# A linear-attention layer: second-half gate rows from stored product forms of x, and keys turned by VectorE and HBM

## The chip, the cores and the metric

The kernel runs on one core of a Trainium2 chip, in one launch. A core has TensorE (PE, matrix products into PSUM), VectorE (DVE), ScalarE (ACT), GpSimd (POOL) and SyncE (SP), which work side by side and wait for each other by semaphores, and DMA queues that move data between HBM and the on-chip SBUF. Times are device microseconds.

## The reference, cut to what matters

One layer of gated linear attention and one squared-ReLU MLP over 1024 tokens of width 1024, all in float32 (`DEPTH` is 1, so the second kind of mixer is not computed).

```
h = rms_norm(x, norm_mix)
q, k, v, r, gk_low = split(h @ w_in)          # 512, 512, 1024, 1024, 16 columns
log_a = log_sigmoid(gk_low @ w_gk_up + b_gk) / 16
# per head (4 heads, 128 key and 256 value columns), in chunks, with a state:
#   b = cumsum(log_a) in the chunk
#   o = (q*exp(b)) @ state + causal(q k^T with decay exp(b_i - b_j)) @ v
#   state = state * exp(b_last) + (k*exp(b_last - b))^T @ v
o = rms_norm(o, g_onorm) * silu(r)
x = x + o @ w_out
x = x + square(relu(rms_norm(x, norm_ffn) @ w_ff1)) @ w_ff2
out = rms_norm(x, final_norm)
```

## The kernel before

**Products by seven forms.** Every large product of float32 is written as three matmuls on a high and a low part: ACT rounds an operand to the high part and DVE subtracts it to give the low part (`split`, lines 79 to 82; in the profile L81 and L82). A 1024 x 1024 by 1024 x 512 product is not formed from eight block products but from seven, of sums and differences of blocks (`form`, lines 149 to 170; the sums are L186). So a plan's entry, for instance "wqk by x", is seven *steps* of 48 matmuls of 128x512 each (`step`, line 234). `PLAIN` is the order in which the seven forms are taken: 0, 5, 1, 2, 3, 4, 6; a position in that order is called *at*, the form's number *n*. Position 5 holds form 4, position 4 holds form 3, and so on. Form 3 of x is its block 22 (second half of the rows of x transposed, second half of the tokens); with the late order that is used here, form 4 of x is block 22 minus block 12. Forms 0 and 5 of x are blocks 11 and 21, the first half of the tokens.

**Plans.** `chunks_of` (line 278) runs three entries: i = 0 is q and k, i = 1 is v, i = 2 is r. While PE works on a step, ACT and DVE make the operands of the next one. `turns` gives the order in which that is done for a position: "x" and "w" are sums, "X" and "W" splits, "n" the sums for the weight side of the position after. `hooks` call other work at a position: `(i, at)` before the next operands are made, `(i, at, "then")` after that and ahead of the step's matmuls, and `(i, at, lane, kp)` between the matmuls of a step.

PE's instructions run in the order in which the program states them. The other engines' order is made by a scheduler at compile time, from priorities (program order, with raised priority for evictions) and estimated times; `order_after(..., wait=False)` fixes an order on one engine. Each engine then works through its own list in order.

**x in other plans.** Plan 0 makes the forms of x; all but 0 and 5 are stored to HBM as high and low parts (`keep`) and loaded again for v and r (`KeptX`, L520).

**PSUM and SBUF.** There are three PSUM banks tagged `mm` and five tagged `gl`. Products of form 5 and of forms 1, 2, 3 use three `mm` banks and one `gl` bank. SBUF tiles come from tagged pools: `big` (8) holds operands, `g4` (6) mixed tiles, `wup` (1) the split of `w_up`.

**The gates.** The gate weights are 16 columns; `split_gate` writes their high and low parts into one 128-column operand, `wgs`, four groups of (high, low), so that one matmul gives all needed partial rows (`gk_rows`, line 449). For the first half of the tokens this is done at (0, 1), from forms 0 and 5 of x: 16 matmuls (`gk_first`), and ACT copies the rows out of their bank (`gk_first_out`, L831). For the second half block 12 of x is loaded again (`x12_load`), scaled and split (`x12_split`, L371 and L374), and 16 matmuls run in plan 1 in two parts at position 5 (`gk_second`). `spread_rms` multiplies the rows by the tokens' norms, `gate_in` multiplies by `w_up`, `gate` and `prep_fast` (L562 to L583) form the cumulative decays and scale q and k by them. POOL copies two small pieces (`top`, L577, and `est`, L581) in each `prep_fast`, and ACT's exponential at L579 overwrites what `top` was copied from.

**The chunks.** After the plans comes a loop over eight chunks of 128 tokens. Chunk c states, in this order: `operands(c + 1)` (q k^T of the next chunk, and the four heads' keys turned by four PE transposes into an `mm` bank, line 657, and split into `kd`), a part of r's last products (`r_part`, L804 and `silu`), `outputs(c)` (L717 to L726), `new_state(c)` (uses `kd`; L696, and POOL's L699) and `outputs_T(c - 1)` (PE transposes of the normed outputs, L736, and ACT's L738). Then come the output projection and the MLP, which the change does not touch. The MLP turns x by DVE blocks of 32x32 and stores to HBM in runs of 128 bytes (`turn_blocks`, L1001, and `turn_store`, L1008).

`general` names a second version of the whole that runs only if the decays are too strong (`flag`); here it does not.

Of the kernel before, what the change touches and what calls it, by code (L numbers as in the profile page):

```python
# [48 lines left out]
def hybrid_trunk(ctx: ExitStack, tc: tile.TileContext, x, xT, w_head, w_r, w_gk, w_up,  # L49
# [15 lines left out]
    def f32(ap):  # L65
        return ap.bitcast(F32)
# [54 lines left out]
    def run(general):  # L121
# [310 lines left out]

        wgr3 = wgr.rearrange("p (k r) -> p k r", r=16)
        wgs5 = wgs.rearrange("p (k g b r) -> p k g b r", k=8, g=4, b=2)
# [14 lines left out]
        def gk_rows(pg, kts, part, start, stop):  # L449

            for kt in kts:
                for hl in range(2):
                    mm(pg, wgs[:, kt * P:(kt + 1) * P], part(kt, hl), start and kt == kts[0] and hl == 0,
                       stop and kt == kts[-1] and hl == 1)
            return pg
# [21 lines left out]
        def qk_into(n, lane, p_):  # L477
            d = qk_view(int(PART[n][0]) - 1, lane)[:, half(int(PART[n][1]) - 1)]
            with tc.high_priority():
                if n in (3, 4, 5):  # L480
                    op = dve.tensor_tensor(d, p_, d, op=ALU.add)
                    if n == 5 and lane:
                        order_after(tc, op, last["s1" if lane == 1 else "s1_low"], wait=False)
                else:
                    op = act.activation(d, p_, AF.Copy)
                    if n == 0:
                        order_after(tc, op, last["split"], wait=False)
# [16 lines left out]
        class KeptX:  # L504
# [9 lines left out]
            def split(self, n):  # L514
                out = self.tiles[n] = [kl(new("big", F32R)) for _ in range(2)]
                for kh in range(2):
                    if n in self.again:
                        split(out[kh][:, :, 0, :], out[kh][:, :, 1, :], xq.blocks["21" if n else "11"](2 * kh, 2))
                    else:
                        nc.sync.dma_start(out[kh].rearrange("p k l t -> p (k l t)").bitcast(F32), xv[n][kh])  # L520
                if n in self.again:
                    keep(n, out)
                return out

        def spread_rms(hf):
# [10 lines left out]
            w_ = new("g4")  # L536
            dg, rbc = w_[:, 512:1024], w_[:, 0:512]
# [3 lines left out]
            raw, gk = box["raw"][hf], box["gk"][:, half(hf)]  # L541
            dst = raw if hf == 0 else dg
            dve.tensor_tensor(dst, raw, rbc, op=ALU.mult)
            act.activation(gk, dst, AF.Copy)
            dve.tensor_tensor(gk[64:128, :], dst[64:128, :], f32(gk[64:128, :]), op=ALU.subtract)
# [26 lines left out]
        def prep_fast(h, hf):  # L572
# [10 lines left out]
            dve.tensor_tensor(kh, a_, kh, op=ALU.mult)  # L583

# [54 lines left out]
        def operands(c, bank_tag="gl"):  # L639
# [15 lines left out]
            kp = new(bank_tag)  # L655
            for h in range(H):
                pe.transpose(kp[:, h * P:(h + 1) * P], qk_view(1, h)[:, c * P:c * P + P], ident)  # L657
# [156 lines left out]
        xq.first = lambda n, kh: scale_x(kh, *{5: ("21",), 1: ("11", "12"), 2: ("22",)}.get(n, ()))  # L814
# [8 lines left out]

        def gk_first():
            pg = gk_rows(new("mm"), range(KT), lambda kt, hl: xlive[0 if kt < 4 else 5][kt % 4 // 2][:, kt % 2, hl, :], True, True)
            box["raw"] = [pg]

        def gk_first_out():
            u, pg = new("g4"), box["raw"][0]
            box["raw"] = [u[:, 0:512]]  # L830
            act.activation(u[:, 0:512], pg, AF.Copy)  # L831

        def x12_load():
            box["x12"] = [new("raw"), new("g4")]
            for kh in range(2):
                nc.sync.dma_start(box["x12"][kh].rearrange("p (k t) -> p k t", k=2), x_piece(2 * kh, 2, 1))

        def x12_split():
            for kh in range(2):
                raw, hi, lo = box["x12"][kh], new("g4", F32R), new("g4" if kh else "raw", F32R)  # L840
                for k in range(2):
                    scaled_split(hi[:, half(k)], lo[:, half(k)], raw[:, half(k)], 2 * kh + k)
                box["x12"][kh] = hi, lo

        def gk_second(part):
            if part == 0:
                box["raw"].append(gk_rows(new("mm"), range(4, KT), lambda kt, hl: xk.tiles[3][kt % 4 // 2][:, kt % 2, hl, :], True, False))
            else:
                gk_rows(box["raw"][1], range(4), lambda kt, hl: box["x12"][kt // 2][hl][:, half(kt % 2)], False, True)
# [13 lines left out]
        hooks = {(0, 1): (gk_first,), (0, 1, "then"): (gk_first_out,), (0, 3): (split_up,),  # L863
                 (0, 4): (g(token_rms, range(0, 4)),), (0, 5): (g(token_rms, range(4, 8)),),
                 (1, 0, 0, 3): (g(spread_rms, 0),),
                 (2, 4): (r_last,),
                 (1, 2): (x12_load,), (1, 4): (x12_split,), (1, 5): (g(gk_second, 0),),
                 (1, 5, 3, 3): (g(gk_second, 1),), (1, 6, 0, 1): (g(spread_rms, 1),)}
        if not general:
            hooks.update({(1, 0, 2, 3): (g(gate_in, 0, 0, "mm"), g(gate_in, 1, 0, "mm")),  # L870
                          (1, 0, 3, 3): (g(gate_in, 2, 0, "mm"),),
                          (1, 1, 0, 1): (g(gate_in, 3, 0, "mm"), g(prep_fast, 0, 0)),
                          (1, 2): (x12_load,),
                          (1, 2, "then"): (g(prep_fast, 1, 0),), (1, 3, "then"): (g(prep_fast, 2, 0),),
                          (1, 4): (), (1, 4, "then"): (g(prep_fast, 3, 0), x12_split),
                          (1, 5): (g(gk_second, 0),),
                          (1, 6, 3, 1): (g(gate_in, 0, 1, "mm"), g(prep_fast, 0, 1)),
                          (2, 0, 0, 0): (g(gate_in, 1, 1, "mm"), g(prep_fast, 1, 1)),
                          (2, 0, 0, 2): (g(gate_in, 2, 1, "mm"),), (2, 0, 1, 0): (g(gate_in, 3, 1, "mm"),),
                          (2, 0, 3, 3): (g(prep_fast, 2, 1),), (2, 3, "then"): (g(prep_fast, 3, 1),),  # L880
                          (2, 4, 2, 1): (g(operands, 0, "mm"),)})
        chunks_of([(wqk, xq, 0, qk_into, PLAIN), (xk, wv, 1, v_into, PLAIN), (xr_, wR, 1, r_into, R_FIRST)], ops_a, hooks, {},
                  turns={(0, 1): ("X", split_gate, "W"), (0, 2): ("x", "X", "w", "W", lambda: last.update(sums=last["split"], s1=last["sum"], s1_low=last["low"]), "n"),
                         (0, 3): ("W", "x", "X", "n"), (2, 3): ("x", "X", "W", g(wR.sums, 3))})

        last_v = box["v"]

# [8 lines left out]
        for c in range(TT):  # L896
            if c == 4 and not general:
# [3 lines left out]
                dve.tensor_scalar(over[:, 1:2], over[:, 0:1], RANGE, None, op0=ALU.is_gt)  # L901
                pf = new("gl")
# [23 lines left out]
            if c:  # L926
                outputs_T(c - 1)

# [311 lines left out]
```

## Time and profile before

| | us |
|---|---|
| median of three runs | 996.23 |
| lowest and highest | 995.94, 997.4 |
| the profiled execution | 996.73 |
| its span in the profile | 995.0 |

The profile shows one execution. A row of a timeline gives start, duration, engine, line, operation, output and input tiles with their shapes and, in square brackets, the idle time of the engine before it and what ended that. Ends of matmuls are modelled, so a row of PE lasts a little longer than the time to the next row's start. L70 is the line of the helper that records every matmul, so that matmuls are told apart by their tiles: `gl<-big,big` and `mm<-big,big` are steps, `mm<-big,g` and `mm<-g,g` or `mm<-raw,g` the gate rows, `mm<-hq,hq` the chunk's q k^T, `gl<-wb,wa` and `gl<-g,hq` its outputs and states. In the chain of waits, a row is a start, a duration and an instruction; "issue" is time in which an engine waited for nothing that the profile shows.

### The profile page before, as it was taken

The numbers are of one execution on the slowest core, as the hardware profiler recorded it, in microseconds if no ns is written. First come the engines' busy times: TensorE is split into PE (matmuls) and PEld (weight loads), VectorE is DVE, ScalarE is ACT, GpSimd is POOL, SyncE is SP. The second block draws the span as 40 slices with busy tenths as digits, with TensorE's granted clock in tenths as the row PEclk, the third lists the DMA queues.
The fourth block names the chain that finished last, engine by engine and source line by source line (L and its number), as shares of the span: only waits on it lengthen the run. The fifth ranks groups of instructions, "written<-read, shape, count | busy, mean of one in ns | idle before, by whom it ended". The sixth has DMA issues, their size and how long they took to land.

```text
span 995.0 us, 12256 instructions
## 1 busy us (share of the span) xinstructions
PE 983.5 (99%) x4508; PEld 820.4 (82%) x4508; DVE 748.7 (75%) x912; ACT 564.1 (57%) x860; POOL 237.0 (24%) x146
## 2 busy tenths in 40 slices
PE   9999999999999999999999999999999999999996
PEld 7788888889988888888888888888888888888885
DVE  5996796768899999699662359974339966569976
ACT  7785564887894376666524446332447433566455
POOL 3000010213440000224042142233133224242270
PEclk9999999999999999999999999999999999999998
DMA  9899786575373257651225993367683225971004
GB/s 271 313 319 380 282 295 215 212 242 196 118 280 108 85 196 312 254 221 33 84 99 206 298 303 89 83 175 260 223 324 100 65 63 212 365 283 49 1 1 173
DMA packets 135693, 193.65 MB, mean 195 GB/s; under 512 B 39240, under 2 KB 100808, under 8 KB 124104
## 3 DMA queue, kind: packets, MB, share of 16 engines
q1 hardware_dynamic: 135064, 192.37, 56.0%
q8 instruction: 37, 0.61, 0.3%
q10 hardware_dynamic: 560, 0.40, 0.1%
q14 instruction: 32, 0.26, 0.1%
HBM read 146.62 MB, written 46.14 MB: 194 GB/s over the span
## 4 chain that ended last, share of the span: by engine, by line
PE 92%; DMA 2%; DVE 2%; ACT 2%; SPq 1%; issue 1%; DVEq 0%; ACTq 0%
PE gl L70 61%; PE mm L70 30%; DMA wb<-in_w_head 1%; DMA wa<-in_w_head 1%; DVE vx L1096 0%; PE mm L657 0%; DVE big L82 0%; ACT g L717 0%; PE mm L736 0%; ACT wb L81 0%; SPq L337 0%; DVE big L804 0%; PE gl L736 0%; DVE g L1137 0%; DVE g L726 0%
## 5 line engine op out<-in xcount | busy, mean ns | idle before, releaser
L70 PE MATMUL gl<-big,big 128*128 128x512 f32 x2700 | 626.4, 389 | 0.7 <-DVE big L82 0.4
L70 PEld LDWEIGHTS gl<-big,big 128*128 128x128 f32 x2700 | 506.5, 188 | 106.5 <-DVE big L82 1.1
L70 PE MATMUL mm<-big,big 128*128 128x512 f32 (+1 forms) x1248 | 291.7, 387 | 0.0
L70 PEld LDWEIGHTS mm<-big,big 128*128 128x128 f32 x1248 | 232.7, 188 | 48.2 <-ACT g L831 0.5
L82 DVE TENSOR_TENSOR big<-wa,big 128x1024 fp32r<-128x1024 f32 (+1 forms) x118 | 155.2, 1335 | 85.6 <-ACT big L81 84.6
L81 ACT ACTIVATE big<-wa 128x1024 fp32r<-128x1024 f32 (+1 forms) x118 | 119.2, 1039 | 127.5 <-PE gl L70 67.0
L186 POOL TENSOR_TENSOR wa<-wa,wb 128x1024 f32<-128x1024 f32 x14 | 42.0, 3011 | 299.9 <-DVE big L82 205.9
L186 POOL TENSOR_TENSOR wa<-wa,wa 128x1024 f32<-128x1024 f32 x28 | 80.0, 2866 | 132.8 <-DVE big L82 132.1
L82 DVE TENSOR_TENSOR big<-wb,big 128x1024 fp32r<-128x1024 f32 x50 | 64.4, 1305 | 27.8 <-ACT big L81 27.8
L81 ACT ACTIVATE big<-wb 128x1024 fp32r<-128x1024 f32 x50 | 51.1, 1054 | 56.8 <-PE gl L70 26.6
L82 DVE TENSOR_TENSOR big<-hq,big 128x1024 fp32r<-128x1024 f32 x48 | 61.5, 1290 | 26.7 <-ACT big L81 26.6
L82 DVE TENSOR_TENSOR big<-raw,big 128x1024 fp32r<-128x1024 f32 x42 | 67.6, 1630 | 4.9 <-ACT big L81 4.9
L81 ACT ACTIVATE big<-hq 128x1024 fp32r<-128x1024 f32 x48 | 48.7, 1052 | 39.4 <-PE gl L70 19.5
L81 ACT ACTIVATE big<-raw 128x1024 fp32r<-128x1024 f32 x42 | 43.4, 1055 | 37.9 <-DVE raw L186 17.8
L186 POOL TENSOR_TENSOR wa<-wb,wa 128x1024 f32<-128x1024 f32 x14 | 41.1, 2947 | 39.7 <-DVE big L82 39.7
L577 POOL COPY top<-g 128x4 f32<-128x4 f32 x8 | 10.1, 1267 | 167.8 <-DVE g L569 167.8
L1030 ACT ACTIVATE hq<-hq 128x1024 f32<-128x1024 f32 x24 | 25.3, 1056 | 40.9 <-DVE hq L1023 40.9
L699 POOL TENSOR_SCALAR g<-g,est 128x256 f32<-128x256 f32 x28 | 29.2, 1059 | 52.2 <-DVE g L696 33.3
L1021 ACT ACTIVATE hq<-gl 128x512 f32<-128x512 f32 x36 | 21.4, 593 | 30.6 <-PE gl L70 30.6
L70 PE MATMUL gl<-wb,wa 128*128 128x256 f32 x180 | 32.1, 310 | 0.0
L1023 DVE TENSOR_TENSOR hq<-gl,hq 128x512 f32<-128x512 f32 x24 | 16.0, 685 | 19.8 <-PE gl L70 19.8
L1068 DVE TENSOR_TENSOR vx<-gl,vx 128x512 f32<-128x512 f32 x44 | 29.1, 679 | 0.9 <-PE gl L70 0.8
(206 smaller groups left out, 898.7 us busy)
## 6 DMA issues: line engine op xcount, KB each, us to landing
big<-xw SPq DMA_DIRECT2D x42, 1024.0 KB, 6.9
big<-xv SPq DMA_DIRECT2D x20, 1024.0 KB, 6.4
xv<-big SPq DMA_DIRECT2D x14, 1024.0 KB, 8.5
xw<-big SPq DMA_DIRECT2D x14, 1024.0 KB, 4.3
wa<-in_w_ff SPq DMA_DIRECT2D x32, 256.0 KB, 4.0
wb<-in_w_ff SPq DMA_DIRECT2D x32, 256.0 KB, 3.9
wa<-in_w_ff SPq DMA_DIRECT2D x16, 512.0 KB, 6.6
wb<-in_w_ff SPq DMA_DIRECT2D x16, 512.0 KB, 5.5
```

The costliest lines, as they stand in the source:

```text
L70: pe.matmul(o, w, m, start=start, stop=stop, skip_group_check=partial)
L81: last["split"] = act.activation(hi, src, AF.Copy)
L82: last["low"] = dve.tensor_tensor(lo, src, f32(hi), op=ALU.subtract)
L186: op = self.eng.tensor_tensor(*(self.ap(b, kp, 2) for b in (o, x_, y_)), op=op)
L577: pool.tensor_copy(top[:, 8 * h + 4 * hf:8 * h + 4 * hf + 4].unsqueeze(2), a[:, :, P - 1:P])
L699: pool.tensor_scalar(S[:, vs], Z[:, vs], g, None, op0=ALU.mult)
L1021: act.activation(d, p_, AF.Copy)
L1023: dve.tensor_tensor(d, p_, d, op=ALU.add)
L1030: act.activation(d2, d2, AF.Relu)
L1068: dve.tensor_tensor(yd, p_, yd, op=ALU.add)
```

## The change

1. *Second-half gate rows.* `x12_load`, `x12_split` and `gk_second` are gone. Since W1 x12 + W2 x22 = (W1 + W2) x22 - W1 (x22 - x12), the rows are formed from the forms 3 and 4 of x that plan 0 holds anyway. `split_gate_again`, called at (0, 4, "then"), makes W1 + W2 and -W1 by two DVE operations on 128x64 values, ordered behind the last low half made by then, and splits them into a second operand. The 16 matmuls stand at (0, 5), ahead of that step's 48.
2. *The copies.* The first gate rows are copied out (`gk_out`) between the scalings of x for position 2, and the four copies of plan 0's first product wait until the x operand of position 2 is split (`qk_first_out`).
3. *Earlier gates.* `spread_rms` for the second half moves from position 6 of plan 1 to its position 0, and `gate_in` and `prep_fast` of both halves move to earlier positions.
4. *The keys.* At the end of each `prep_fast` DVE transposes the scaled keys in 32x32 blocks (128x512) into the tile of the decays. Four DMAs, begun by GpSimd one or more positions later, store it to HBM in runs of 128 bytes, so that a row there is a token with 512 values. A chunk's 128 rows are loaded by SyncE into the one `wup` tile; `operands` splits that, and its four PE transposes and their `mm` bank are gone.
5. The reduction of `top` moves from chunk 4 to chunk 2.

```diff
-        def split_gate():
+        def split_gate(wgs, wgr3):
+            wgs5 = wgs.rearrange("p (k g b r) -> p k g b r", k=8, g=4, b=2)
             for g in range(4):
                 split(wgs5[:, :, g, 0, :], wgs5[:, :, g, 1, :], wgr3)
+
+        def split_gate_again():
+            t = wgu[:, 128:256]
+            for op in (dve.tensor_tensor(t[:, 0:64], wgr[:, 0:64], wgr[:, 64:128], op=ALU.add),
+                       dve.tensor_scalar(t[:, 64:128], wgr[:, 0:64], -1.0, None, op0=ALU.mult)):
+                order_after(tc, op, last["low"], wait=False)
+            box["wgs"] = new("g4", F32R)
+            split_gate(box["wgs"], t.rearrange("p (k r) -> p k r", r=16))
...
+        def gk_out(hf):
+            if hf == 0:
+                box["raw"] = new("g4")
+            act.activation(box["raw"][:, half(hf)], box["pg"], AF.Copy)
...
-                    op = act.activation(d, p_, AF.Copy)
-                    if n == 0:
-                        order_after(tc, op, last["split"], wait=False)
+                    act.activation(d, p_, AF.Copy)
+
+        def qk_first_out():
+            for d, p_ in box["q0"]:
+                order_after(tc, act.activation(d, p_, AF.Copy), last["split"], wait=False)
...
             dve.tensor_tensor(kh, a_, kh, op=ALU.mult)
+            turn_keys(h, hf, a_)
...
+        def turn_keys(h, hf, u):
+            dve.transpose(u, qk_view(1, h)[:, half(hf)])
+            kmoved[h, hf] = u
+
+        def store_keys(h, hf):
+            u = kmoved.pop((h, hf))
+            for q_ in range(4):
+                dst = km[hf * 512:hf * 512 + 512, h * P + 32 * q_:h * P + 32 * q_ + 32].rearrange("(b i) j -> i b j", i=32)
+                pool.dma_start(dst, u[32 * q_:32 * q_ + 32, :].rearrange("p (b j) -> p b j", j=32))
+
+        def load_keys(c):
+            krows[c] = new("wup")
+            box["keys"] = nc.sync.dma_start(krows[c], km[c * P:(c + 1) * P, :])
...
-            kp = new(bank_tag)
-            for h in range(H):
-                pe.transpose(kp[:, h * P:(h + 1) * P], qk_view(1, h)[:, c * P:c * P + P], ident)
+            if general:
+                kp = new(bank_tag)
+                for h in range(H):
+                    pe.transpose(kp[:, h * P:(h + 1) * P], qk_view(1, h)[:, c * P:c * P + P], ident)
+            else:
+                kp = krows.pop(c)
...
-        hooks = {(0, 1): (gk_first,), (0, 1, "then"): (gk_first_out,), (0, 3): (split_up,),
-                 (0, 4): (g(token_rms, range(0, 4)),), (0, 5): (g(token_rms, range(4, 8)),),
-                 (1, 0, 0, 3): (g(spread_rms, 0),),
-                 (2, 4): (r_last,),
-                 (1, 2): (x12_load,), (1, 4): (x12_split,), (1, 5): (g(gk_second, 0),),
-                 (1, 5, 3, 3): (g(gk_second, 1),), (1, 6, 0, 1): (g(spread_rms, 1),)}
+        hooks = {(0, 1): (lambda: gk_rows(wgs, (xlive[0], xlive[5])),),(0, 3): (split_up,), (0, 4, "then"): (split_gate_again,),
+                 (0, 4): (g(token_rms, range(0, 4)),), (0, 5): (g(token_rms, range(4, 8)), lambda: gk_rows(box["wgs"], (xlive[3], xlive[4]))),
+                 (0, 5, "then"): (g(gk_out, 1),),
+                 (1, 0, 0, 3): (g(spread_rms, 0),), (1, 0, 1, 3): (g(spread_rms, 1),),
+                 (2, 4): (r_last,)}
...
+            for i, at, f in ((1, 1, (store_keys, 0, 0)), (1, 2, (store_keys, 1, 0)), (1, 3, (store_keys, 2, 0)), (1, 4, (store_keys, 3, 0)),
+                             (1, 6, (store_keys, 0, 1)), (2, 0, (store_keys, 1, 1)), (2, 1, (store_keys, 2, 1)), (2, 2, (store_keys, 3, 1)),
+                             (2, 2, (load_keys, 0))):
+                hooks[i, at, "then"] = (g(*f), *hooks.get((i, at, "then"), ()))
...
+            if c + 2 < TT and not general:
+                load_keys(c + 2)
```

More of the change, by code (lines that the diff above doesn't have):

```diff
@@ L447, in run, with gk_rows @@
         box = {}
-        def gk_rows(pg, kts, part, start, stop):
-            for kt in kts:
+        def gk_rows(wgs, forms):
+            box["pg"] = new("mm")
+            for kt in range(KT):
                 for hl in range(2):
-                    mm(pg, wgs[:, kt * P:(kt + 1) * P], part(kt, hl), start and kt == kts[0] and hl == 0,
-                       stop and kt == kts[-1] and hl == 1)
-            return pg
+                    mm(box["pg"], wgs[:, kt * P:(kt + 1) * P], forms[kt // 4][kt % 4 // 2][:, kt % 2, hl, :],
+                       kt + hl == 0, kt + hl == KT)
+        def gk_out(hf):
+            if hf == 0:
+                box["raw"] = new("g4")
+            act.activation(box["raw"][:, half(hf)], box["pg"], AF.Copy)
         def token_rms(ts):
@@ L519, in split @@
                     else:
-                        nc.sync.dma_start(out[kh].rearrange("p k l t -> p (k l t)").bitcast(F32), xv[n][kh])
+                        last["xv"] = nc.sync.dma_start(out[kh].rearrange("p k l t -> p (k l t)").bitcast(F32), xv[n][kh])
                 if n in self.again:
@@ L535, in spread_rms @@
                 mm(pb, ones_r, u[:, half(l)], l == 0, l == 1)
-            w_ = new("g4")
-            dg, rbc = w_[:, 512:1024], w_[:, 0:512]
+            rbc = new("g4")[:, 0:512]
             act.activation(rbc, pb, AF.Copy)
@@ L540, in spread_rms @@
                 box["gk"] = new("g4", F32R)
[L541 to L545, printed above, removed]
+            raw, gk = box["raw"][:, half(hf)], box["gk"][:, half(hf)]
+            dve.tensor_tensor(raw, raw, rbc, op=ALU.mult)
+            act.activation(gk, raw, AF.Copy)
+            dve.tensor_tensor(gk[64:128, :], raw[64:128, :], f32(gk[64:128, :]), op=ALU.subtract)
         def chunks(ap):
@@ L812, in run, with x_first @@
         xq_split = xq.split
-        xq.first = lambda n, kh: scale_x(kh, *{5: ("21",), 1: ("11", "12"), 2: ("22",)}.get(n, ()))
+        def x_first(n, kh):
+            if (n, kh) == (1, 1):
+                gk_out(0)
+            scale_x(kh, *{5: ("21",), 1: ("11", "12"), 2: ("22",)}.get(n, ()))
+        xq.first = x_first
         def remember(n):
@@ L822, in run @@
         xk, xr_ = KeptX((0, 5)), KeptX()
[L824 to L849, printed above, removed]
         wv = weight_side(True, from_v, dve, late=True)
@@ L869, in run @@
         if not general:
             hooks.update({(1, 0, 2, 3): (g(gate_in, 0, 0, "mm"), g(gate_in, 1, 0, "mm")),
[L871 to L880, printed above, removed]
+                          (1, 0, 3, 3): (g(gate_in, 2, 0, "mm"), g(prep_fast, 0, 0)),
@@ L884, in run @@
                          (0, 3): ("W", "x", "X", "n"), (2, 3): ("x", "X", "W", g(wR.sums, 3))})
         last_v = box["v"]
+        if not general:
+            load_keys(1)
         for t in range(4):
@@ L896, in run @@
         for c in range(TT):
-            if c == 4 and not general:
+            if c == 2 and not general:
                 over = new("st")
@@ L901, in run @@
                 dve.tensor_scalar(over[:, 1:2], over[:, 0:1], RANGE, None, op0=ALU.is_gt)
+            if c == 4 and not general:
                 pf = new("gl")
```

12 lines of the change are left out of this document (10 added, 2 removed).

## The prediction

> **What bounds the kernel now.** I read the page first, then the busy time by stretches, the timelines of the engines around each place that the change touches, and the chain of waits. All times are microseconds.
>
> ```profile
> span 995.0 us, 12256 instructions
> PE 983.5 (99%) x4508; PEld 820.4 (82%) x4508; DVE 748.7 (75%) x912; ACT 564.1 (57%) x860; POOL 237.0 (24%) x146
> ...
> PE 92%; DMA 2%; DVE 2%; ACT 2%; SPq 1%; issue 1%; DVEq 0%; ACTq 0%
> ```
>
> TensorE (PE) carries 92% of the chain that ends last. A change can gain only by taking instructions off PE, or by ending one of its few waits; it loses wherever PE waits for something new. So I look at the stretches in which another engine is nearly as full.
>
> ```profile
> 33.00:66.00 33.00, 32.65 (x145) 26.83 (x144) 32.89 (x33) 25.75 (x38) 0.00 (x0) 1.00 0.82 314
> ...
> 128.00:160.00 32.00, 32.00 (x143) 26.51 (x142) 27.23 (x44) 14.78 (x22) 3.76 (x7) 1.00 0.90 297
> ...
> 260.00:300.00 40.00, 39.80 (x258) 35.62 (x257) 36.28 (x81) 35.28 (x96) 16.79 (x16) 1.00 0.66 225
> ```
>
> The columns are the stretch, its length, then busy time and count of PE, weight load, VectorE (DVE), ScalarE (ACT) and GpSimd (POOL), the granted clock, the DMA share and GB/s. The clock is 1.00 in all three, so it plays no part. From 33 to 66, in the q and k projection, DVE is busy for 32.89 of 33.00. From 128 to 160, in the v projection, only DMA is near its limit (0.90). From 260 to 300, in the attention's chunks, DVE and ACT are at nine tenths. These three places decide the matter.
>
> **The start (6 to 34).** The change puts the copy of the first gate rows ahead of the scaling of two x blocks, and the four copies of q's and k's first product behind them, on ACT.
>
> ```profile
> 17.77 3.79 PE L70 MATMUL mm<-big,g 128*128 128x512 f32 x16
> ...
> 22.75 4.58 PE L70 MATMUL mm<-big,big 128*128 128x512 f32 x18
> ...
> 28.56 4.24 PE L70 MATMUL mm<-big,big 128*128 128x512 f32 x18
> 32.64 0.61 PE L70 MATMUL gl<-big,big 128*128 128x512 f32 x2
> 33.61 1.19 PE L70 MATMUL gl<-big,big 128*128 128x512 f32 x4 [0.35 <-DVE big L82]
> ...
> 65.93 24.64 PE L70 MATMUL gl<-big,big 128*128 128x512 f32 x108
> ```
>
> The last row gives the pace: 24.64 / 108 = 0.228 a matmul, so 48 of them, one step, take 10.95, and 16 gate rows 3.65. Against that pace two waits stand here. The 18 at 22.75 take 4.58 where the 18 at 28.56 take 4.24: 0.34, spent on the third `mm` bank, which holds the gate rows until ACT copies them. Between 32.64 and 33.61 two matmuls need 0.46 of 0.97: 0.51 of waiting for the low half of a weight operand on DVE.
>
> ```profile
> 20.65 2.04 ACT L485 ACTIVATE hq<-gl 128x512 f32<-128x512 f32 x4
> 22.56 2.57 ACT L366 ACTIVATE vx<-vx,vec 128x512 f32<-128x512 f32 x4
> ```
>
> ```profile
> 24.00 2.44 DVE L186 TENSOR_TENSOR raw<-vx,vx 128x1024 f32<-128x1024 f32 x2 [1.62 <-issue]
> ...
> 32.34 2.35 DVE L82 TENSOR_TENSOR big<-wa,big 128x1024 fp32r<-128x1024 f32 x2
> ```
>
> DVE idles 1.62 until the first two scalings (L366) are through; these stood behind the four copies (L485, 2.04). With the copies behind, DVE starts up to 1.62 earlier, its low halves at 32.34 come earlier too, and the bank is copied some 2 earlier. Both waits go: up to 0.85 gained, at least 0 if the weight blocks' landing holds DVE anyway. I take 0.8. The copies go into a gap of ACT; what comes next late is at 65.93.
>
> **The second gate rows (at 65.93).** Sixteen matmuls leave the v projection, and sixteen stand ahead of the step that starts at 65.93: PE's count is unchanged. Removed as well are a reload of 1 MB of x and its four scalings and four low halves, none of which PE waited for. New is a wait. The second set of gate weights is formed by two small DVE operations, which are ordered behind the last low half of this step's x operand, then four ACT copies and four DVE subtractions; PE cannot pass the gate rows to begin the step.
>
> ```profile
> 65.38 1.22 DVE L82 TENSOR_TENSOR big<-vx,big 128x1024 fp32r<-128x1024 f32 x1
> ```
>
> ```profile
> L81 ACT ACTIVATE g<-g 128x128 fp32r<-128x128 f32 x4 | 0.9, 294 | 0.0
> ...
> L82 DVE TENSOR_TENSOR g<-g,g 128x128 fp32r<-128x128 f32 x4 | 0.9, 277 | 0.0
> ```
>
> Before, the step could begin at 65.93 on the first half of the operand, with the second half (65.38 to 66.60) still in the making. Now PE waits for 66.60, plus about 0.5 for the two operations of half that width (bounded by 277 ns each), plus 0.9 for the copies, plus 0.28 for the last subtraction: 68.3, a wait of 2.3. If DVE is 1.62 ahead from the start and PE 0.85, it is 2.3 - 1.62 + 0.85 = 1.5. I take the middle, 1.9. The bounds: 0, if DVE gets so far ahead that its evictions and this operand are done before PE; 3.5, if one more low half (1.22) is put ahead of the small ones. Behind the waiting PE nothing else is late: each following step has 3.65 more time for its operands. On ACT the four copies hold up the squares of x's rows, which are needed only by the v projection.
>
> **The keys (96 to 220).** Eight DVE block transposes, 32 stores begun by GpSimd and eight loads on SyncE's queue are added; 32 PE transposes go.
>
> ```profile
> L1001 DVE STREAM_TRANSPOSE g<-g 128x1024 f32<-128x1024 f32 x8 | 9.9, 1236 | 3.1 <-DMA g<-xh 3.1
> ```
>
> ```profile
> L1008 SPq DMA_DIRECT2D xm<-g x32: 302/563/4391, 543.5 to 704.0; - x32
> ```
>
> ```profile
> xm<-g SPq DMA_DIRECT2D x32, 128.0 KB, 7.5
> ...
> raw<-xv SPq DMA_DIRECT2D x16, 256.0 KB, 3.4
> ```
>
> A transpose of half that width costs about 0.62, eight of them 5.0 of DVE, in a stretch where DVE has 4.8 free of every 32 (128 to 160) and where the low halves just removed gave time back: hidden. The stores have the form of the later `xm` stores, runs of 128 bytes, half as many each. No GpSimd store is in this trace. From SyncE's issue it would be 0.56 (0.30 to 4.39); from GpSimd's own copies in this stretch up to 3.98 (row below). I take 1.3 each, nearer to SyncE's row, so about 5 for the four of a head, inside a step of 10.95. Queued behind them on POOL are the copies of `top` and `est`, and ACT's next exponential waits for the former.
>
> The stores' bytes meet the kept x operands on the DMA engines:
>
> ```profile
> L520 SPq DMA_DIRECT2D big<-xv x2: 339/522/705, 139.9 to 143.7; - x2
> ...
> DMA to landing us min/median/max: 7.0/7.2/7.5
> ```
>
> ```profile
> 158.00 1.52 PE L70 MATMUL gl<-big,big 128*128 128x512 f32 x6
> ```
>
> These loads, begun by 143.7, have landed by 151.2, and the step that needs them starts at 158.00. That is 6.8 of cover, about as much as a load takes; while it holds, the stores cost nothing, and without it a load twice as slow would cost 0.7 a step. The key loads (256 KB like `raw<-xv`, 3.4) have one buffer: the next starts when the last is split, in a chunk of some 9.7. Hidden, if they land within 6.
>
> **The chunks (220 to 299).** Here PE loses its work.
>
> ```profile
> L657 PE MATMUL mm<-ident,hq 128*128 128x128 f32 x32 | 4.9, 276 | 0.1
> ```
>
> ```profile
> 272.26 0.74 ACT hq L738 x2
> 273.00 0.04 issue
> 273.04 0.66 PE mm L657 x4
> ...
> 282.77 0.44 PE mm L657 x4
> ...
> 296.73 1.58 DVE g L726 x4
> 298.31 0.04 issue
> 298.36 0.33 PE mm L736
> ```
>
> On the chain, four transposes take 0.44 where they run freely; eight groups make 3.5. At 273.04 they take 0.66, because their `mm` bank came late from ACT (L738); such waits, 0.2 at two places, go with the bank: 3.9 in all. Not all of it need arrive. The stretch ends with PE waiting for DVE's normed outputs (L726, to 298.31), and DVE's round is as long as PE's:
>
> ```profile
> 266.67 0.69 DVE L804 TENSOR_TENSOR big<-mm,big 128x512 f32<-128x512 f32 x1 [0.39 <-PE mm L70]
> ...
> 270.15 0.75 DVE L749 SCALAR_TENSOR_TENSOR big<-big,tok 128x512 f32<-128x512 f32 x1 [1.20 <-ACT big L748]
> ...
> 276.82 0.68 DVE L804 TENSOR_TENSOR big<-mm,big 128x512 f32<-128x512 f32 x1
> ```
>
> One round of DVE, 266.67 to 276.82, is 10.15 with 1.20 of idle for ACT in it; PE's, 273.04 to 282.77, is 9.73. PE's becomes 9.3. DVE can follow as far as its idle time, 0.39 and 1.20 a round, was PE's doing. I take 3.2, nearer to the full 3.9 since each round holds more idle than the 0.44 asked for; the least is 1.3, three early chunks at 0.44, if the later ones keep DVE's pace. The key's split reads SBUF instead of PSUM:
>
> ```profile
> L81 ACT ACTIVATE wb<-vx 128x512 fp32r<-128x512 f32 x16 | 10.2, 635 | 0.0
> ...
> L81 ACT ACTIVATE wa<-mm 128x512 fp32r<-128x512 f32 x8 | 4.7, 588 | 0.0
> ```
>
> That is 0.05 more a chunk on ACT, off PE's path.
>
> **The sum.** -0.8 + 1.9 - 3.2 = -2.1. The profiled execution took 996.73 (span 995.0 and 1.7 around it), so 994.6; it lies 0.5 above the median of 996.23, from which the change gives 994.1. About 0.2%, 2.0, is what a measurement of this kernel can tell from no change: under 994.2 counts as faster, over 998.2 as slower.
>
> **The rivals.** First, DVE holds the chunks: the loop gives only 1.3, and the sum is -0.8 + 1.9 - 1.3 = -0.2, 996.0, no change. For it speaks the chain's end on L726 at 298.31; against it DVE's idle time in each round. Second, the gate weights come as late as they can (3.5) while the loop gives all: -0.8 + 3.5 - 3.9 = -1.2, 995.0, no change either; with the weak loop and no gain at the start it is 0 + 3.5 - 1.3 = +2.2, 998.4, slower. Third, and slower by much: the stores hold up POOL.
>
> ```profile
> 184.42 3.98 POOL L577 COPY top<-g 128x4 f32<-128x4 f32 x1 [1.67 <-DVE g L569]
> ```
>
> This copy of 128x4 values lasts 3.98, while DVE runs operations without a pause. If each store takes as long, four take 15.9 of a step of 10.95; the next head's `top` copy is 5.0 later at each of six heads, ACT stops at its exponential with the next weights' splits behind it, and PE is late by 6 x 5.0 less the 6.8 of cover: 996.2 - 2.1 + 23.2 = 1017. It decides from 10.95 / 4 = 2.7 a store on. Against it: it was one copy in sixteen, and a store reads no SBUF values with GpSimd. [...]
>
> **How the numbers follow.** The forecast, with the loop's gain near 3.2 and the wait near 1.9 or less, has 0.47 and is faster; its own range is 991.5 to 994.2. No change by either way has 0.33. Slower has 0.20: 0.12 for POOL's stores, 0.08 for the late weights with a weak loop. The range of 991.5 to 998.5 goes from the best of all bounds (-0.85 + 0 - 3.9 = -4.75) to the 998.4 of the second rival, and leaves out POOL's case and a few mishaps.
>
> **What would show it.** Right: 18 matmuls in 4.24 at 22.75 and no wait at 33; a gap of PE between 65 and 68, ended by DVE's 128x128 subtractions; no L657 rows outside the fallback, a chunk of 9.3 to 9.5, and the end of the chunks some 3 earlier than the shifts at the start and at 65.93 alone would put it; POOL's stores well under 2.7 each. Wrong: PE idle between 96 and 220, ACT waiting for POOL at L579 by several microseconds, or DVE and ACT waiting in the chunks for the landing of keys.

## The result and the profile after

| us | before | after |
|---|---|---|
| median (5 runs each) | 996.23 | 1001.57 |
| lowest and highest | 995.7, 997.4 | 1000.17, 1003.05 |
| the profiled execution | 996.73 | 1002.46 |
| its span | 995.0 | 1000.7 |

The ratio is 1.0053, with a 95% interval of 1.0039 to 1.0068. The change made the kernel slower by 5.3, where 2.1 faster was forecast; 1001.57 is outside the forecast's range of 991.5 to 998.5. First the page of the kernel after:

```profile
span 1000.7 us, 12293 instructions
PE 980.9 (98%) x4476; PEld 817.4 (82%) x4476; DVE 750.4 (75%) x922; ACT 562.9 (56%) x861; POOL 259.0 (26%) x178
...
PE 87%; DVE 5%; ACT 2%; DMA 2%; issue 1%; SPq 1%; DVEq 0%; ACTq 0%
```

TensorE has its 32 instructions less and is busy 2.6 less than before (983.5), yet it carries only 87% of the chain that ends last, and DVE has 5% in place of 2%. So TensorE waits for something new. Its timeline names the places (start, duration, shapes, count, idle time before and what ended it):

```profile
17.75 4.16 PE L70 MATMUL mm<-big,g 128*128 128x512 f32 x16
...
23.12 4.24 PE L70 MATMUL mm<-big,big 128*128 128x512 f32 x18
...
33.73 1.20 PE L70 MATMUL gl<-big,big 128*128 128x512 f32 x4 [0.47 <-DVE big L82]
...
61.97 4.24 PE L70 MATMUL mm<-big,big 128*128 128x512 f32 x18
69.55 5.53 PE L70 MATMUL mm<-big,g 128*128 128x512 f32 x16 [3.34 <-DVE g L82]
74.91 5.38 PE L70 MATMUL gl<-big,big 128*128 128x512 f32 x23
...
103.94 0.51 PE L70 MATMUL mm<-g,ones_r 128*128 128x512 f32 x1 [0.96 <-DVE g L553]
...
267.54 0.38 PE L70 MATMUL gl<-st,ones 128*128 128x1 f32 x2 [1.42 <-DVE g L735]
```

The 18 matmuls at 61.97 are through, at 0.228 each, at 66.07; before, the step began at 65.93. The second gate rows begin only at 69.55: a gap of 3.5. And the 16 rows reach to 74.91, 5.36 where 16 x 0.228 = 3.65 was due. The busy time by stretches says why (length, PE, weight load, DVE, ACT, POOL, then the granted clock):

```profile
66.00:69.50 3.50, 0.21 (x1) 0.00 (x0) 3.50 (x11) 1.86 (x5) 0.00 (x0) 1.00 1.04 382
69.50:75.00 5.50, 5.45 (x17) 4.35 (x18) 3.17 (x3) 2.12 (x2) 0.00 (x0) 0.69 0.97 362
75.00:96.00 21.00, 21.00 (x95) 17.38 (x94) 14.36 (x33) 12.63 (x20) 0.00 (x0) 1.00 0.88 334
```

In the gap PE is busy for 0.21 of 3.50 and DVE for all of it; in the 5.5 behind it the granted clock is 0.69, then 1.00 again. The rows are slow because the clock is.

The chunk loop did gain. Its length is the time from the first q k^T of chunk 0 to the first matmul of the output projection, before and after:

```profile
220.59 1.05 PE L70 MATMUL mm<-hq,hq 128*128 128x128 f32 x8
...
298.88 11.14 PE L70 MATMUL gl<-big,big 128*128 128x512 f32 x48
```

```profile
227.15 1.05 PE L70 MATMUL mm<-hq,hq 128*128 128x128 f32 x8
...
302.45 11.14 PE L70 MATMUL gl<-big,big 128*128 128x512 f32 x48
```

78.29 became 75.30. So the two executions differ thus: 0.1 at the start, 3.5 of gap, 1.7 of slow rows, 1.0 at 104 and 0.3 not assigned make the 6.56 by which the loop starts later. The loop gives back 2.99, net of the new wait of 1.42 at 267 that stands in it; 3.57 remain and stay. The last outputs are issued 3.58 apart, by ScalarE's queue, before and after:

```profile
988.92 0.38 ACTq L1129 DMA_DIRECT2D out_y<-hq  x1
```

```profile
992.50 0.38 ACTq L1150 DMA_DIRECT2D out_y<-hq  x1
```

But the spans end at 995.0 and 1000.7: 6.1 and 8.2 behind those issues. Another 2.1 arise where no engine computes. 6.56 - 2.99 + 2.1 = 5.7, the difference of the spans.

### The profile page after: what moved, and what is told of

It is laid out like the page before. It is cut to its first block, busy times and chain, and to the rows that moved or that the text cites. A ratio compares the mean times of both kernels' runs of the same rounds, so it can differ in the third digit from the quotient of the medians.

```text
span 1000.7 us, 12293 instructions
## 1 busy us (share of the span) xinstructions
PE 980.9 (98%) x4476; PEld 817.4 (82%) x4476; DVE 750.4 (75%) x922; ACT 562.9 (56%) x861; POOL 259.0 (26%) x178
## 4 chain that ended last, share of the span: by engine, by line
PE 87%; DVE 5%; ACT 2%; DMA 2%; issue 1%; SPq 1%; DVEq 0%; ACTq 0%
PE gl L70 59%; PE mm L70 28%; DVE big L82 2%; DMA wb<-in_w_head 1%; ACT big L81 1%; DVE wa L186 0%; DVE vx L1117 0%; DMA vec<-in_vecs 0%; DMA vx<-in_xT 0%; DVE hq L496 0%; ACT g L756 0%; DVE raw L186 0%; PE mm L775 0%; SPq L337 0%; DVE g L765 0%
## 5 line engine op out<-in xcount | busy, mean ns | idle before, releaser
L594 POOL COPY top<-g 128x4 f32<-128x4 f32 x8 | 11.2, 1399 | 123.0 <-DVE g L586 123.0
```

The lines of the kernel that those rows point to most:

```text
L594: pool.tensor_copy(top[:, 8 * h + 4 * hf:8 * h + 4 * hf + 4].unsqueeze(2), a[:, :, P - 1:P])
```

## The experiments

My theory: TensorE's gap for the second gate weights and the low clock behind it cost 5.2, the late spreading of the norms (L553, at 104) costs 1, the keys gain 3 in the loop, and the end costs 2.1. The rival: the keys' stores and loads cost the time, and the gap would only move.

**e1: the second gate weights one step earlier.**

```diff
-        hooks = {... (0, 4, "then"): (split_gate_again,),
+        hooks = {... (0, 3, "then"): (split_gate_again,),
...
```

> One change to the kernel after: the second gate weights are formed one step earlier, behind step (0,3)'s operands. Theory: TensorE stood idle from 66.05 to 69.55 for these weights and ran the 16 gate rows behind it at a granted clock of 0.67 (5.36 us in place of 3.65); with the weights there early no wait is left at 66 and the rows take 3.65, so about 5 us less than the kernel after: 996 to 997. Rival (the loss lies in GpSimd's stores and the keys' traffic): the wait goes, but DVE's late halves only move it, and the time stays near 1001.5.

Measured: 998.96, ratio 1.0027 (1.0017 to 1.0036). TensorE's timeline of e1:

```profile
65.02 3.87 PE L70 MATMUL mm<-big,g 128*128 128x512 f32 x16
...
98.34 0.51 PE L70 MATMUL mm<-g,ones_r 128*128 128x512 f32 x1 [1.77 <-DVE g L553]
99.95 0.50 PE L70 MATMUL mm<-g,ones_r 128*128 128x512 f32 x1 [1.10 <-DVE g L553]
100.29 4.49 PE L70 MATMUL gl<-big,big 128*128 128x512 f32 x12
```

The gap at 66 is gone and the rows run at full pace: that part of the theory holds. But most of the gain is lost again at 98, since TensorE now arrives earlier and DVE does not: the diagonal blocks for the second spreading are 1.77 and 1.10 late, and the 12 matmuls behind them take 4.49 in place of 12 x 0.228 = 2.7. That is 4.6 where the kernel after lost 0.96, so only 1.5 of the 5.2 is left; another 2.0 goes at the end, where the span closes 6.2 behind the last issue in place of 8.2. The stretches of e1 show the clock at work a second time:

```profile
96.60:100.30 3.70, 0.86 (x3) 0.50 (x4) 3.25 (x11) 1.32 (x2) 0.00 (x0) 1.00 0.74 312
100.30:104.80 4.50, 4.50 (x14) 3.56 (x13) 1.38 (x2) 1.23 (x2) 0.00 (x0) 0.62 0.01 5
```

**e2: the gap filled with work.**

```diff
+            wgu_s = first_wgs
...
             box["pg"] = new("mm")
+            for _ in range(fill):                      # 15 at (0, 5)
+                mm(box["pg"], wgu_s[:, 0:P], forms[0][0][:, 0, 0, :], True, True)
...
```

> The kernel after with 15 added matmuls, whose product is thrown away, ahead of the second gate rows: TensorE works through the 3.4 us in which it stood idle at 66 to 69.5, and the weights come no earlier. Theory (the low clock behind the gap is the answer to the gap): the 16 gate rows start near 69.5 as before, take 3.65 in place of 5.36, no slice shows a granted clock below 0.95, and the time is 1.7 less, near 1000. Rival (the clock is lowered for another reason, such as the load at that place): the slice at 70 to 75 still shows 0.67, the time stays at 1001.5 or grows.

Measured: 1000.41, ratio 1.0043 (1.003 to 1.0057). The 15 and the 16 in e2's timeline, and the clock behind:

```profile
64.67 7.50 PE L70 MATMUL mm<-big,g 128*128 128x512 f32 x31
```

```profile
69.50:75.00 5.50, 5.50 (x26) 4.55 (x25) 2.36 (x2) 5.50 (x9) 0.00 (x0) 1.00 1.00 378
```

The next step begins at 72.01, so 31 matmuls take 7.34, 0.237 each, at a clock of 1.00. The same place, about the same load, no idle time: no slow clock. The low clock is the answer to the gap. From the end of the step before to the start of the next one it is 7.34 in place of 8.84 (66.07 to 74.91), 1.5 less. The medians differ by 1.2, but the intervals of the two ratios overlap.

**e5: early weights, and the second spreading later.**

```diff
+        hooks = {... (0, 3, "then"): (split_gate_again,),   # as in e1
...
-                 ... (1, 0, 1, 3): (g(spread_rms, 1),),
...
-                          (1, 0, 3, 3): (g(gate_in, 2, 0, "mm"), g(prep_fast, 0, 0)),
+                          (1, 0, 3, 3): (g(spread_rms, 1), g(gate_in, 2, 0, "mm"), g(prep_fast, 0, 0)),
...
```

> e1_early_weights with the second spreading of the norms (spread_rms(1)) two lanes later in step (1,0), behind lane 3 in place of lane 1. Theory: what held e1 back from its 5 us are the two waits for that spreading's diagonal blocks (1.77 and 1.10 at 98 to 100) and the lower clock behind them (12 matmuls in 4.49 in place of 2.9), 4.4 together; with the matmuls asked for later both waits and the slow stretch go: 998.96 - 4.4 = 994.5, between 994 and 996, ahead of the kernel before. Rival (the blocks are late however late they are asked for, or e1's distance has another cause): 998 to 999.

Measured: 994.44, ratio 0.9978 (0.9969 to 0.9987). The second gate rows follow the step at once, and the next wait of TensorE behind the one at 33 is at 261:

```profile
65.97 3.91 PE L70 MATMUL mm<-big,g 128*128 128x512 f32 x16
...
261.10 0.38 PE L70 MATMUL gl<-st,ones 128*128 128x1 f32 x2 [1.33 <-DVE g L735]
```

With two hooks moved the same change is faster than the kernel before, by 2.1. Against the kernel after, the profiled executions agree up to the 18 matmuls ahead of the gate rows (61.88 and 61.97). From there to the loop e5 takes 6.3 less, near the 5.2 and 1.0 of the theory; the loop is as long, and the end is 2.0 shorter (6.2 in place of 8.2), for which the theory has no reason.

**e10: the later spreading alone**, with the weights late as in the kernel after.

```diff
-                 ... (1, 0, 1, 3): (g(spread_rms, 1),),
...
-                          (1, 0, 3, 3): (g(gate_in, 2, 0, "mm"), g(prep_fast, 0, 0)),
+                          (1, 0, 3, 3): (g(spread_rms, 1), g(gate_in, 2, 0, "mm"), g(prep_fast, 0, 0)),
...
```

> The kernel after with only the second spreading of the norms moved to behind lane 3 of step (1,0); the gate weights stay late. Theory: the wait of 0.96 at 104 goes and nothing else: 1 less than the kernel after, near 1000.5; the gap at 66 to 69.5 and the granted clock of 0.67 behind it stay. Rival (the two places are one, the late norms are what the gap causes): as the kernel after, within 0.4, or all 5 gone.

Measured: 1000.83, ratio 1.0036 (1.0023 to 1.0049). The wait at 104 is gone, the gap and the slow rows stay:

```profile
70.59 5.51 PE L70 MATMUL mm<-big,g 128*128 128x512 f32 x16 [3.35 <-DVE g L82]
```

The two places are separate in the kernel after; they are coupled only in that mending the first uncovers the second.

**e4 and e7: without the keys' part.** e4 is the kernel after, e7 is e5, in both TensorE turns the keys as before:

```diff
-            turn_keys(h, hf, a_)
...
-                kp = krows.pop(c)
+            kp = new(bank_tag)
+            for h in range(H):
+                pe.transpose(kp[:, h * P:(h + 1) * P], qk_view(1, h)[:, c * P:c * P + P], ident)
```

> The kernel after without the keys' part: TensorE turns the keys in the chunk loop as in the kernel before, nothing is turned by DVE, stored or loaded; start, gate rows and hooks stay as in the kernel after. Theory: the chunk loop loses its gain of about 3, the wait of the flag's matmul (1.4) goes, the tail falls from 8.2 to 6.1: 1001.5 + 3 to 4.5 - 2.1 = 1002.5 to 1004. Rival (the keys' traffic is what costs): faster than the kernel after, 997 to 999.

> e5_early_late without the keys' part: TensorE turns the keys, and nothing is stored by GpSimd. Only the gate rows of the second half and the start differ from the kernel before. Theory: with the waits mended the gate rows cost and bring nothing in TensorE's time, and the tail is 6.1 to 6.3: 996.4, within 1 of the kernel before. Rival (forming the second weights and reordering the start cost DVE and ACT time that lands on the path elsewhere): 998 or more.

Measured: e4 1002.58, ratio 1.0061 (1.0047 to 1.0074); e7 997.28, ratio 1.0005 (0.9996 to 1.0014). The loop in e4 and in e5:

```profile
226.81 1.05 PE L70 MATMUL mm<-hq,hq 128*128 128x128 f32 x8
...
304.89 11.18 PE L70 MATMUL gl<-big,big 128*128 128x512 f32 x48
```

```profile
220.75 1.05 PE L70 MATMUL mm<-hq,hq 128*128 128x128 f32 x8
...
296.01 11.14 PE L70 MATMUL gl<-big,big 128*128 128x512 f32 x48
```

78.08 with TensorE's transposes, 75.26 without; the medians of e7 and e5 differ by 2.8, just as much. So the keys' part is worth 2.8 in the loop and its traffic costs TensorE nothing that shows; the rival falls. The gate rows' part, once its waits are mended, costs and brings nothing (e7).

**e8: the keys' part alone**, added to the kernel before; the second gate rows are formed as before, from the reloaded block 12, and the gates come later, so that the stores stand one or two positions later than in the kernel after.

```diff
             dve.tensor_tensor(kh, a_, kh, op=ALU.mult)
+            turn_keys(h, hf, a_)
...
+            else:
+                kp = krows.pop(c)
```

> The kernel before with the keys' part alone: DVE turns the keys, GpSimd stores them, SyncE loads them, TensorE turns none; gate rows and start stay as in the kernel before. Theory: the chunk loop gains 3 (or 4 where the flag's wait does not appear), against up to 2.1 in the tail of some executions: 993 to 995. Rival (the keys' traffic costs more than the loop gains): 996.5 or more.

Measured: 1000.48, ratio 1.0042 (1.0029 to 1.0056), against my expectation. Where e8 loses it, in the rows of ACT, DVE and PE and in the stretches:

```profile
140.42 1.34 ACT L371 ACTIVATE g<-raw,vec 128x512 fp32r<-128x512 f32 x2 [2.81 <-DMA km<-g]
...
159.91 1.41 DVE L374 SCALAR_TENSOR_TENSOR g<-g,vec,g 128x512 fp32r<-128x512 f32 x2
...
160.71 1.65 PE L70 MATMUL mm<-g,g 128*128 128x512 f32 x3 [2.68 <-DVE g L374]
```

```profile
160.70:165.50 4.80, 4.50 (x11) 3.24 (x12) 4.80 (x12) 0.00 (x0) 0.00 (x0) 0.64 0.30 126
```

TensorE waits 2.68 for the last two low parts of the reloaded block (L374), and a third time a lower clock follows (0.64). The loop is 75.95 long, so the keys' gain is there, but it starts at 226.32 in place of 220.59. Why the low parts are late is only in part shown. A turned key sits in a `g4` tile until its store has landed, and the reloaded block's high parts (L371) need `g4` tiles too: ScalarE waits 2.81 for a store at 140. But TensorE is held up by no more than 0.21 there, and the low parts that it waits for stand late in DVE's own list, at 159.91 where the kernel before has its last at 144.27, behind weight sums and evictions. Whether the scheduler put them there for want of tiles was not tested, nor whether later hooks would mend it, as they mended e1. What the times show is that neither part alone is faster than the kernel before (e7, e8) and both together are (e5), which the prediction did not see.

**e3: the stores begun by SyncE.**

```diff
-                pool.dma_start(dst, u[32 * q_:32 * q_ + 32, :].rearrange("p (b j) -> p b j", j=32))
+                nc.sync.dma_start(dst, u[32 * q_:32 * q_ + 32, :].rearrange("p (b j) -> p b j", j=32))
```

> The kernel after with the 32 stores of the turned keys begun by SyncE in place of GpSimd. Theory: the 2.1 us by which the span ends later behind the last output's issue (8.2 against 6.1) belong to the queue that GpSimd opens: the tail is 6.1 again, 2 us less, near 999.5, if SP's queue does not hold up the loads behind stores that wait for DVE. Rival (the tail has another reason): the tail stays at 8.2 and the time near 1001.5 or, where loads are held up, above it.

Measured: 1023.14, ratio 1.0272 (1.0256 to 1.0288). The tail is 6.1 again (last issue 1012.58, span 1018.7), but TensorE waits for operands again and again in the v and r plans, for up to 2.3. The scheduler gave ScalarE and DVE another order there, so that the test is not a clean one; what the queue alone costs stays open.

**e6 and e9: the flag's wait (1.42 at 267).** e6 takes another bank, e9 moves the matmul from chunk 4 to behind the outputs of chunk 7; both on top of e5.

```diff
-                pf = new("gl")
+                pf = new("mm")                         # e6
...
             outputs(c)
+            if c == TT - 1 and not general:            # e9
+                pf = new("gl")
```

> e5_early_late with the flag's matmul in a bank of the other group (mm in place of gl). Theory: the wait of 1.3 to 1.4 at 266 is for a gl bank that DVE's scaling of the outputs still reads, so it goes: 1.3 less than e5, near 993.2. Rival (the wait only moves to the next matmul that needs the bank): as e5, within 0.4.

> e5_early_late with the flag's matmul moved from the start of chunk 4 to behind the outputs of chunk 7. Theory: at chunk 4 it takes over the gl bank of the outputs that DVE still scales and waits 1.3; behind the last outputs its bank is that of a state sum, long free, and nothing needs one soon: no wait, 994.4 - 1.3 = 993.1. Rival (the loop's length is set by DVE, not by this wait): as e5, within 0.4.

Measured: e6 994.16, ratio 0.997 (0.996 to 0.998); e9 993.23, ratio 0.9964 (0.9951 to 0.9977). In e6 the wait moves to the next user of the bank:

```profile
263.31 3.01 PE L70 MATMUL mm<-big,raw 128*128 128x512 f32 x12 [1.47 <-DVE flag L923]
```

In e9 it is gone, but the loop of e9 is as long as that of e5 (219.71 to 295.10, 75.39, against 75.26):

```profile
219.71 1.05 PE L70 MATMUL mm<-hq,hq 128*128 128x128 f32 x8
...
293.40 1.50 PE L775 MATMUL mm<-ident,g 128*128 128x128 f32 x4 [0.60 <-DVE g L765]
...
295.10 11.14 PE L70 MATMUL gl<-big,big 128*128 128x512 f32 x48
```

The two rows hide an exchange. The round with the flag in it (from one q k^T to the next) falls from 10.83 in e5 to 9.09 in e9, like most rounds beside it; but the stretch from the last q k^T to the projection, where the matmul now stands, grows from 16.43 to 17.81, and TensorE waits there for DVE's normed outputs. So the rival, that DVE sets the loop's length, does not follow. The wait does cost what it lasts: in e2 and e13 it happens to be 0.32 and 0.78, and their loops are 74.17 and 74.63. e9 is the fastest kernel of the study, 3.7 less than the kernel before beside it (996.96). But the 1.2 between its median and that of e5 is not from the loop, and the intervals of the two ratios overlap; its profiled execution reached the loop 1.04 earlier than e5's, which has a wait of 0.93 at 33, and ended 0.2 sooner. What makes up the 1.2 stays open.

**The end.** e11 is the kernel after once more.

> The kernel after once more, unchanged, for a second profile of its end. In the first the span ended 8.2 behind the issue of the last output, in the kernel before 6.1, in e1, e5, e6 and e8, which store by GpSimd as well, 6.2 to 6.4, in e2 8.3. Theory A (it differs from one execution to the next): some other figure between 6.1 and 8.3. Theory B (it belongs to this program, as it is laid out): 8.2 again. Either way 1001.5 in time.

Measured: 1002.14, ratio 1.0053 (1.004 to 1.0066), and a tail of 8.2 again (992.05 to 1000.3). So it is no accident of one execution. The DMA traffic of the last microseconds, as a strip of 40 slices, of the kernel after from 996.9 to 1000.7 and of e1 from 995.1 to 996.9:

```profile
DMA  0206000000000000000000000000020000000000
...
q14 instruction: 4, 0.03, 2.6%
```

```profile
DMA  0000760000000000000000000000000000000000
```

All that moves there is instructions, in pieces of 8 KB. In the kernel after the last piece comes alone at 999.7, 2.4 behind the one before, and the span ends 1.0 later; in e1 the last two come together at 995.3, and the span ends 1.6 later. Such a late last piece stands in all eight long ends, 2.1 to 2.5 behind the one before; in e3 and e7, with 6.1 and 6.7, it is 1.3 and 1.1. It is not one piece more: behind the last issue 8 of them come in the kernel after and 7 each in the kernel before, e1 and e10, and e10's end is long (8.3). I tried to move it by the length of the code: e12 adds 12 small instructions to each of VectorE, ScalarE and GpSimd late in the kernel after; e13, e14 and e15 lengthen the branch that is never run.

```diff
+            for m, e in enumerate((dve, act, pool)):   # e12, at load_gfin
+                pad = sb.tile([P, 1], F32, name=f"pad{m}{int(general)}")
+                for _ in range(12 if not general else 1):
+                    if e is act:
+                        act.activation(pad, one, AF.Copy)
+                    else:
+                        e.memset(pad, 0.0)
...
+        for _ in range(32):                            # e13; 64 in e14, 96 in e15
+            dve.memset(pads[0], 0.0)
+            act.activation(pads[1], one, AF.Copy)
+            pool.memset(pads[2], 0.0)
+            mm(spare[:, 0:1], ones, one, True, True)
         run(True)
```

> The kernel after with 12 added instructions on one element a partition on each of VectorE, ScalarE and GpSimd at the start of the last chunk of the feed-forward part, where they compute nothing that is used. Theory (the 2 us at the end of the kernel after hang on the length of the engines' programs, so that a few more instructions of any kind change them): the span ends 6.1 to 6.9 behind the last output's issue in place of 8.2, and the time falls to 1000. Rival (they hang on the order of the work, which is as in the kernel after): 8.2 again, 1001.5 to 1002.5.

> The kernel after with 32 small instructions for each of TensorE, VectorE, ScalarE and GpSimd added in the branch that is never run. Theory (the fourth fetch of instructions behind the last output hangs on where the code after the branch lies): at one or two of the three lengths 32, 64 and 96 the fetch at the end goes and the span ends 6.1 to 6.9 behind the last issue, 999.5 in time. Rival (it does not hang on that): 8.2 at all three, 1001.5 to 1002.

> As e13, with 64 instructions for each engine. Theory: 6.1 to 6.9 at one or two of the three lengths, with the time 2 less. Rival: 8.2 at all three.

> As e13, with 96 instructions for each engine. Theory: 6.1 to 6.9 at one or two of the three lengths, with the time 2 less. Rival: 8.2 at all three.

Measured: 1003.73, 1000.74, 1002.3 and 1001.5, with tails of 8.3, 8.2, 8.1 and 8.1. None of these lengths changes it. The tail is 8.1 to 8.3 in all eight profiles that have both GpSimd's stores and the late weights (after, e2, e10, e11, e12 to e15), and 6.1 to 6.9 in the others. Why, stays open.

## Why the prediction was wrong

**The start (-0.8): did not come.** The 18 matmuls do take 4.24, as forecast, but the gate rows ahead of them now take 3.99 to the next row (17.75 to 21.74), and the wait at 33 stays (0.47). DVE's sums of x do start 0.93 earlier (23.07 in place of 24.00), but then DVE waits for weights and x from HBM, in the kernel after:

```profile
28.38 1.23 DVE L186 TENSOR_TENSOR wa<-wa,wb 128x1024 f32<-128x1024 f32 x1 [0.25 <-DMA wa<-in_w_head]
30.12 1.23 DVE L186 TENSOR_TENSOR wa<-wa,wb 128x1024 f32<-128x1024 f32 x1 [0.51 <-DMA vx<-in_xT]
```

It is the case "0 if the weight blocks' landing holds DVE anyway", which the text named and did not take. One execution is too little to size it: the 18 matmuls at 61.97 begin between 60.59 and 62.99 in the fifteen profiles that have the new start, at 61.7 on the mean, and at 61.85 and 61.88 in the two with the old one (before, e8).

**The second gate rows (+1.9): this step failed.** It measured 3.5 of gap and 1.7 of slow rows, 5.2 in all. The rows of DVE, and one of ACT, in the kernel after show how the gap comes about:

```profile
64.90 1.22 DVE L82 TENSOR_TENSOR big<-vx,big 128x1024 fp32r<-128x1024 f32 x1
66.03 0.68 DVE L496 TENSOR_TENSOR hq<-mm,hq 128x512 f32<-128x512 f32 x1
66.63 0.22 DVE L445 TENSOR_TENSOR g<-g 128x64 f32<-128x64 f32 x1
66.77 0.19 DVE L446 TENSOR_SCALAR g<-g 128x64 f32<-128x64 f32 x1
66.87 1.22 DVE L82 TENSOR_TENSOR big<-wb,big 128x1024 fp32r<-128x1024 f32 x1
67.27 0.89 ACT L81 ACTIVATE g<-g 128x128 fp32r<-128x128 f32 x4
68.00 0.68 DVE L496 TENSOR_TENSOR hq<-mm,hq 128x512 f32<-128x512 f32 x1
68.60 0.89 DVE L82 TENSOR_TENSOR g<-g,g 128x128 fp32r<-128x128 f32 x4
```

My sum added up the chain of the gate weights alone. DVE's list has three more rows in it: an eviction (0.68) ahead of the two small operations, and behind them, while ACT makes the copies, a low half of the weight operand (1.22) and a second eviction (0.68). The four subtractions then come in one go, 0.89, where my sum had the last of them alone (0.28). That the gap equals the upper bound, 3.5, is luck: the bound had the low half in it and not the rest, and took the x operand for ready at 66.60, where it was ready at 66.12. In a stretch where DVE is busy for 32.89 of 33.00, which the prediction itself showed, a chain that goes from DVE to ACT and back must be given what else stands in DVE's list.

The second mistake is the sentence "The clock is 1.00 in all three, so it plays no part". It was read from a profile in which the longest wait of TensorE is 1.1; a change that adds a longer one can change the clock, and here it did: it is 1.00 in the gap, 0.58 from 69.5 to 72, 0.78 from 72 to 75 and 1.00 again behind that (the kernel after). e2 shows that the gap is the cause, by filling it: 1.00 in all these stretches. What sets how far the clock falls, and when it comes back, no run shows; from 69 to 75 it is 0.72 in the kernel after, e11 and e15, 0.50 in e14 and 1.00 in e13. Nine profiles have the gap, of 3.30 to 3.36 (the kernel after, e3, e4 and e10 to e15). The rows behind it take 5.30 to 5.54 in six of them, and in e3 the clock from 66 to 75 is 0.81, as in the kernel after and e4; in e13 and in e14 the rows take this:

```profile
68.60 3.92 PE L70 MATMUL mm<-big,g 128*128 128x512 f32 x16 [3.35 <-DVE g L82]
```

```profile
70.01 6.63 PE L70 MATMUL mm<-big,g 128*128 128x512 f32 x16 [3.36 <-DVE g L82]
```

3.92 in one, 6.63 in the other, 5.53 in the kernel after, against 3.87 without a gap (e1): the same wait costs nothing, 1.7 or 2.8 beyond itself. Shorter waits were followed by a lower clock too. In e1 it was 1.77 and 1.10 with a matmul between them (0.62 behind), and in e3 a single wait of 2.30 (at 184.95): the 53 matmuls behind it take 13.85 to the next row, where 53 x 0.228 = 12.1 was due, and the granted clock from 128 to 220 is 0.96.

**"Behind the waiting PE nothing else is late": wrong.** The second spreading was moved from position 6 of the v plan to position 0, and no term of my sum had it. It waits 0.96 in the kernel after and 2.9, with a slow clock (0.62) on top, once the first gap is gone (e1).

**The keys (0): right.** TensorE waits for nothing between 105 and 220. The third rival fell: all GpSimd's store issues of the kernel after in one row (durations in ns: least, median, most):

```profile
L615 POOL DMA_DIRECT2D km<-g x32: 648/648/856, 122.0 to 200.0; - x32
```

0.65 each where 2.7 was the point from which it decides, and half of the 1.3 that I took, under a DVE that is busy for 72.22 of the 92.00 from 128 to 220. Their 2.10 MB went over a DMA queue of their own, as the prediction's argument against the rival supposes:

```profile
q0 software_dynamic: 1024, 2.10, 0.8%
```

A copy of `top` of 3.98 is there again (L594, at 125.89), and no store takes over 0.86: what lengthens that copy does not show on the stores, and what it is, no run shows.

**The chunks (-3.2): the mechanism was right, the number in part luck.** It measured -3.0 (75.30 against 78.29), and -2.8 between e4 and the kernel after. But the rounds fall to 9.1, not to the 9.3 to 9.5 of the forecast: DVE follows without holding anything back. What brings the sum down to 3.0 is the flag's wait, 1.42, which the loop before does not have and which no term of mine held; with 0.32 of it (e2) the loop gives 4.1, more than the full 3.9.

**The end (+2.1): not in the sum.** Nothing in the trace of before speaks of it, and its cause is open.

So the second rival had the right wait, late gate weights of 3.5. Its 998.4 needed a weak loop as well, which did not come: with the start, the gap and the loop as measured (0.1 + 3.5 - 3.0) the sum gives 996.8. The low clock (1.7), the moved spreading (1.0), the end (2.1) and the 0.3 not assigned make up the rest, to 1001.9.

## What to carry to other kernels

Where an engine is full, the time of a chain through it is the time of its whole list, not of the chain's own links (a gap of 3.5 here, where the links were given 1.9); so make a small operand that TensorE will need one step earlier than looks necessary. An idle time of TensorE of some 3 us can cost nearly twice itself, by the clock that follows (3.36 and then 2.8 in e14, at a clock of 0.50; nothing beyond the 3.35 in e13), and a wait that is mended often uncovers the next (e1), so mend and look again. Try the parts of a change alone and together: neither was faster alone (e7 the same, e8 slower), and together they were (e5).

## What the runs showed of the hardware

- A gap of TensorE of 3.30 to 3.36 was followed by slow matmuls in eight of nine profiles (16 of them in 5.30 to 6.63 in seven, where 3.9 was due; a clock of 0.81 from 66 to 75 in e3) and by none in one (e13, 3.92, at 1.00). A single wait of 2.30 (e3) was followed by 53 matmuls in 13.85 where 12.1 was due, a gap of 1.77 and 1.10 broken by a matmul (e1) by a granted clock of 0.62; waits of 0.96 and 1.42 (the kernel after, at 104 and 267) by 1.00.
- Stores of 64 KB in runs of 128 bytes took GpSimd 0.65 each to begin (at most 0.86), beside a DVE that was busy for 78% of 128 to 220.
- The span ended 6.1 to 6.9 behind the last DMA issue in some programs and 8.1 to 8.3 in others. In the long ends a last 8 KB piece of instructions comes 2.1 to 2.5 behind the one before and the span closes about 1 behind it; what sets its time is open.
